# Four gate products in a row ahead of the latent attention, and sums of x formed later

## The chip, the core and the metric

The kernel runs on one core of a Trainium2 chip. The metric is the device time of one execution in microseconds (us), the median of several runs. TensorE (PE) multiplies; VectorE (DVE), ScalarE (ACT) and GpSimd (POOL) work beside it; SyncE (SP) issues the transfers of weights.

## What is computed

A trunk of two layers on 256 tokens of width 2048, all in float32. `u` is a normed copy of `x`, and `w_in` gives all the projections of a layer in one matrix: the latents of the latent attention (MLA), its rotary key, the queries, keys and values of a neighbourhood attention (NA), and two gates of width 2048.

```python
u = rmsnorm(x, norm_mix[l])
c_q, c_kv, k_pe, q_na, k_na, v_na, gate_a, gate_b = jnp.split(u @ w_in[l], IN_SPLITS, axis=-1)
y_a = mla_attention(...) @ w_o_mla[l]          # from c_q @ w_uq, c_kv @ w_ukv, k_pe
y_b = neighbourhood_attention(...) @ w_o_na[l]
merged = jax.nn.sigmoid(gate_a) * y_a + jax.nn.sigmoid(gate_b) * y_b
x = x + merged @ w_out[l]
h = rmsnorm(x, norm_mlp[l]) @ w_ff1[l]
x = x + jnp.square(jax.nn.relu(h)) @ w_ff2[l]
```

A final norm follows the second layer.

## The kernel before

**Weights and products.** Weights come as strips of up to 1 MB, tile `raw`, three buffers, issued by SyncE. Each strip is split into a rounded high part (`hi`, a cast on ScalarE, L176, L200) and the remainder (`lo`, a subtraction on VectorE, L177, L201); a product of two numbers is then three matmuls, high by high, high by low and low by high. Activations are split in the same way into a tile `pair` (L165 on ScalarE; L167 or L169 on VectorE). `gemm_a` (matmuls L231 to L233) and `gemm_b` (L222, L223) are plain products. `gemm_s` (L399) is a product with a Strassen scheme: strips numbered j in `pairs` are merged, with seven products of blocks in place of eight; the others are plain. A merged strip needs sums of the weights (tile `sums`, L445, L448 and L449 on VectorE) and sums of the activations, which `sums_of` makes by four additions of 128 columns (L348 to L351); `forms` (L353) calls it and splits the result (L358 on ScalarE, L359 on VectorE). A `gemm_s` ends with eight additions of banks (L464, VectorE) after a copy (L465 on ScalarE). Its matmuls are L413.

**What sets the order.** Every engine runs its own list in order; a tile framework waits for data and for buffers. Work that is not a step of a product (softmax heads, norms, transpositions, sums) sits in generators. `start(gen, lag)` puts one in `pending`, to be continued `lag` ticks later; `tick()`, called after every few matmuls, continues one that is due, or takes a head from `queued` when six ticks have passed since the last. `drain()` continues them all; `gemm_s` calls it at its first merged strip. `have()` continues the pending work until an activation exists. The scheduling of the framework then fixes the place of each instruction on its engine.

**A layer.** First half: the NA queries, keys and values; the latents C_Q and C_KV; the rotary key; the first gate product of gate b, here GB0 (1024 columns, `gemm_s`), the first two of the four products of `w_o_na` (512 columns each, `gemm_a`), GB1, the other two. Then the MLA stage: four rounds of `w_uq` and `w_ukv`, each of which queues two heads; the rotation is L516. Then GA0 (strips in the order LATE, three merged ones in a row), two products of `w_o_mla`, GA1, the other two. After each of these four a block of merged rows is complete (L777 and L778) and `turned` transposes it (matmuls L483), splits it and, for merged strips, calls `forms`. Second half: `w_out` as two `gemm_s`, then the feed-forward part, which ends with two `gemm_a` whose results are added to `x` (L866) and squared for the next norm (L328). At the end of a layer, and in layer 0's first product, `turned` does for `x` what it does for the merged rows.

**Buffers.** The two halves open and close pools of their own (`wpool`, `tmp`), so the second half's larger `hi` and `lo` tiles lie where the first half's were. In the first half the sums of the weights use the tag `pp`, two buffers, which the heads of attention use too (L548, L549).

Of the kernel before, what the change touches and what calls it, by code (L numbers as in the profile page):

```python
# [33 lines left out]
F32 = mybir.dt.float32  # L34
# [5 lines left out]
P = 128  # L40
# [27 lines left out]
MIXED, MERGED = (1, 2, 3), (1, 2, 3)  # L68
EARLY, LATE = [0, 4, 1, 5, 2, 6, 3, 7], [0, 4, 5, 6, 1, 3, 2, 7]

# [5 lines left out]
def trunk(ctx: ExitStack, tc: tile.TileContext, x, w_in, w_uq, w_ukv, rpb, w_o_mla, w_o_na,  # L76
# [3 lines left out]
    slots = ctx.enter_context(tc.tile_pool(name="slots", bufs=NSLOT))  # L80
    keep = ctx.enter_context(tc.tile_pool(name="keep", bufs=2))
    psum = ctx.enter_context(tc.tile_pool(name="psum", bufs=8, space=bass.MemoryType.PSUM))

    tmp = wpool = None
    hbufs, smalls, strips = HBUFS, SMALL, False
# [94 lines left out]
    def weights(w, nk, c0, n, before=None):  # L180
# [3 lines left out]
        for k0 in range(0, nk, 2):  # L184
            if before:
                before(k0)
            if k0 % step == 0:
                raw = wpool.tile([P, 2048], F32, tag="raw", name="raw", bufs=RBUFS)
                raw = raw[:, :step * n].rearrange("p (k n) -> p k n", n=n)
                nc.sync.dma_start(raw, w[k0 * P:(k0 + step) * P, c0:c0 + n].rearrange("(k p) n -> p k n", p=P))  # L190
                if strips:
                    his, los = (t.rearrange("p (k n) -> p k n", n=n) for t in parts(raw.rearrange("p k n -> p (k n)")))
# [11 lines left out]
    def weights_twice(w, nk, c0, n):  # L204

        raw = wpool.tile([P, 2048], F32, tag="raw", name="raw", bufs=RBUFS)
        raw = raw[:, :nk * n].rearrange("p (k n) -> p k n", n=n)
# [145 lines left out]

    def forms(f, sums, j):

        s = sums_of(f)
        h, lw = pair(), pair()
        nc.scalar.copy(h, s)  # L358
        nc.vector.tensor_tensor(lw, s, h.bitcast(F32), op=ALU.subtract)  # L359
        sums[j] = h, lw  # L360
        return
        yield

# [35 lines left out]
    def gemm_s(w, c0, get, order, pairs, evac):  # L399
# [23 lines left out]
        for j in order:  # L423
            raw = wpool.tile([P, 2048], F32, tag="raw", name="raw", bufs=RBUFS)
            nc.sync.dma_start(raw.rearrange("p (k n) -> p k n", n=1024),
# [13 lines left out]
            if strips:  # L439
                whole_ts = wpool.tile([P, 2048], F32, tag="sums", name="sums", bufs=1)  # L440
                ts = whole_ts[:, :1024], whole_ts[:, 1024:]
            else:
                ts = [tmp.tile([P, 1024], F32, tag="pp", name="sums", bufs=2) for _ in range(2)]
# [32 lines left out]
    def turned(src, c4, dst, scale, sums, pairs):  # L476


        for c in range(0, 4, 2):
# [18 lines left out]
            if j in pairs:  # L498
                start(forms(f, sums, j), 8)
            yield 1  # L500
# [124 lines left out]
    norm = RowNorm()  # L625
    xg, xs4 = [None] * NC, [None] * (NC // 2)

# [4 lines left out]
    def enter(k0):  # L632
# [4 lines left out]
        if k0 % 4 == 0:  # L637
            enter.gen = turned_x(k0 // 4, xg, G_MIX, xs4)
        next(enter.gen)
# [6 lines left out]
    for l in range(DEPTH):  # L646
# [43 lines left out]
        gemm_b(wi, C_Q, xg, latent(cq, nq, G_QA + 4 * l))  # L690
        start(nq.scales(), 10)
        gemm_b(wi, C_KV, xg, latent(ckv, nkv, G_KVA + 4 * l))
        start(nkv.scales(), 10)
# [8 lines left out]

        part = {}

        def gate(th):
            def evac(r):
                for i in range(2):
                    for t in range(2):
                        nc.scalar.activation(r[t, i], r[t, i], AF.Tanh, scale=mix.half[:, t:t + 1])
                th.update(r)  # L710
            return evac

        mixed = blocks(xg, xs4, MIXED)
        for g in range(2):
            th = {}
            gemm_s(wi, C_GB + g * 1024, mixed, EARLY, MIXED, gate(th))
            for i in range(2):
                def merge(t, ps):
                    m = part[t, 2 * g + i] = th[t, i]
                    nc.vector.scalar_tensor_tensor(m, m, 1.0, ps, op0=ALU.add, op1=ALU.mult)  # L720

                gemm_a(w_o_na[l], (2 * g + i) * 512, att_na, merge)

# [44 lines left out]

        mg, ms4 = [None] * NC, [None] * (NC // 2)
        for g in range(2):  # L770
            th = {}
            gemm_s(wi, C_GA + g * 1024, mixed, EARLY if g else LATE, MIXED, gate(th))
            for i in range(2):
                def merge(t, ps):
                    c4 = 2 * g + i
                    m, h = part[t, c4], th[t, i]
                    nc.vector.scalar_tensor_tensor(h, h, 1.0, ps, op0=ALU.add, op1=ALU.mult)  # L777
                    nc.vector.tensor_tensor(m, m, h, op=ALU.add)  # L778
                    if t == 1:
                        start(turned(lambda t: part[t, c4], c4, mg, lambda c: 0.5, ms4, MERGED), 2)  # L780

                gemm_a(w_o_mla[l], (2 * g + i) * 512, att, merge)
        half_a.close()
# [19 lines left out]
        for g in range(2):  # L803
# [10 lines left out]

            gemm_s(w_out[l], g * 1024, blocks(mg, ms4, MERGED), EARLY, MERGED, residual)
        mlp.scale()
# [12 lines left out]
        for b in range(NB):  # L829
# [31 lines left out]
            if b == NB - 1:  # L861
                rows = [[v[2 * k:2 * k + 2] for v in h] for h in hid for k in range(2)]
                for c4 in range(2, 4):
# [6 lines left out]
                    gemm_a(w2, c4 * 512, rows, residual3)  # L870
        xg, xs4 = nxt, nxt4
        if not last:
# [70 lines left out]
```

## Time and profile before

| | |
|---|---|
| median of 3 runs | 2681.57 us (2680.39 to 2682.54) |
| profiled execution | 2678.33 us |
| its span, first to last instruction | 2676.6 us |
| share of the span: TensorE, VectorE, ScalarE, GpSimd | 98%, 79%, 55%, 4% |
| mean granted clock of TensorE | 0.996 |
| moved by DMA | 508.95 MB, mean 190 GB/s |

In a row of a timeline stand the start in us, the length in us, engine, line, operation and output<-input tiles; in brackets the engine's idle time before it and what ended that. A matmul's length holds its latency too, so lengths overlap, and the pace is read from start to start. In a row of the list of waits stand the total, the number of waits and the longest. In a row of a window stand its bounds, its length, the busy time of PE, PE's weight loads, DVE, ACT and POOL with their counts, the granted clock of PE, the share of the DMA engines and GB/s. In a row of a group stand the count, then busy time and mean ns of one, then the idle time before.

### The profile page before, as it was taken

How to read it: one execution, taken by the hardware profiler on the slowest of the kernel's cores; microseconds unless marked ns; L12 is line 12 of the kernel's file. 1: busy time of each engine (PE TensorE's matmuls, PEld its weight loads, DVE VectorE, ACT ScalarE, POOL GpSimd, SP SyncE). 2: the span in 40 equal slices, each digit the busy share in tenths (PEclk: the TensorE clock that was granted, in tenths of full speed). 3: DMA queues.
4: the chain of work that ended last, by engine and by line, in shares of the span. 5: the costliest groups of instructions: out<-in, count | busy, mean ns of one | idle time of the engine just before them, and what ended most of it. 6: DMA issues, size and time to landing. Idle time of an engine off the chain costs nothing.

```text
span 2676.6 us, 32005 instructions
## 1 busy us (share of the span) xinstructions
PE 2624.5 (98%) x12498; PEld 2187.4 (82%) x12498; DVE 2126.3 (79%) x2496; ACT 1464.3 (55%) x1719; POOL 94.7 (4%) x117
## 2 busy tenths in 40 slices
PE   8999999999999999999999999999999999999998
PEld 6888887877888888888888888878788888888886
DVE  6778787878888887888767787978888888878885
ACT  6555565546554545545545555645565555455553
POOL 0100000000000010000001000000000000100000
PEclk9999999999999999999999999999999999999999
DMA  7555544565567575675555555445555665756744
GB/s 229 175 169 185 195 157 140 194 196 174 195 200 236 163 242 193 204 231 176 197 173 174 167 189 197 147 152 179 191 189 189 206 218 187 236 206 190 252 168 145
DMA packets 175256, 508.95 MB, mean 190 GB/s; under 512 B 13696, under 2 KB 18176, under 8 KB 175104
## 3 DMA queue, kind: packets, MB, share of 16 engines
q1 hardware_dynamic: 166192, 490.08, 55.0%
q0 software_dynamic: 8768, 16.78, 3.2%
q8 instruction: 98, 1.61, 0.2%
q14 instruction: 54, 0.44, 0.0%
q10 hardware_dynamic: 144, 0.04, 0.0%
HBM read 492.18 MB, written 2.10 MB: 185 GB/s over the span
## 4 chain that ended last, share of the span: by engine, by line
PE 68%; issue 21%; DVE 6%; ACT 3%; POOL 1%; DMA 1%; SPq 0%; POOLq 0%; ACTq 0%; DVEq 0%
PE bank L413 40%; PE bank L222 8%; PE bank L231 4%; PE bank L233 4%; PE bank L232 4%; PE bank L223 4%; DVE lo L177 3%; ACT hi L176 3%; PE bank L382 1%; DVE sums L445 1%; PE bank L238 1%; PE bank L237 1%; PE bank L236 1%; DMA raw<-in_w_in 1%; POOL xt L854 1%
## 5 line engine op out<-in xcount | busy, mean ns | idle before, releaser
L413 PE MATMUL bank<-hi,pair 128*128 128x512 f32 x5156 | 1614.8, 392 | 16.6 <-ACT hi L176 15.6
L413 PEld LDWEIGHTS bank<-hi,pair 128*128 128x128 f32 x5156 | 967.6, 188 | 229.8 <-ACT hi L176 32.9
L413 PE MATMUL bank<-lo,pair 128*128 128x512 f32 x2578 | 1010.6, 392 | 4.2 <-DVE lo L177 4.0
L176 ACT CAST hi<-raw 128x2048 fp32r<-128x2048 f32 (+3 forms) x416 | 633.3, 1534 | 435.0 <-PE bank L413 290.9
L177 DVE TENSOR_TENSOR lo<-raw,hi 128x2048 fp32r<-128x2048 f32 (+3 forms) x416 | 754.0, 1819 | 132.2 <-ACT hi L176 130.3
L413 PEld LDWEIGHTS bank<-lo,pair 128*128 128x128 f32 x2578 | 485.3, 188 | 110.0 <-DVE lo L177 11.4
L177 DVE TENSOR_TENSOR lo<-sums,hi 128x2048 fp32r<-128x2048 f32 (+1 forms) x134 | 255.9, 1910 | 162.3 <-ACT hi L176 161.9
L201 DVE TENSOR_TENSOR lo<-raw,hi 128x1024 fp32r<-128x1024 f32 (+1 forms) x224 | 270.2, 1213 | 134.0 <-ACT hi L200 133.1
L176 ACT CAST hi<-sums 128x2048 fp32r<-128x2048 f32 (+1 forms) x134 | 214.8, 1603 | 288.1 <-DVE sums L449 201.5
L222 PE MATMUL bank<-pair,hi 128*128 128x512 f32 x960 | 346.4, 403 | 9.7 <-ACT hi L200 6.0
L200 ACT CAST hi<-raw 128x1024 fp32r<-128x1024 f32 (+1 forms) x224 | 230.0, 1035 | 206.5 <-PE bank L222 81.1
L223 PE MATMUL bank<-pair,lo 128*128 128x256 f32 x960 | 267.8, 283 | 0.8 <-DVE lo L201 0.8
L222 PEld LDWEIGHTS bank<-pair,hi 128*128 128x128 f32 x960 | 181.3, 189 | 50.1 <-ACT hi L200 7.0
L232 PE MATMUL bank<-lo,pair 128*128 128x512 f32 (+1 forms) x576 | 218.1, 379 | 0.0
L233 PE MATMUL bank<-hi,pair 128*128 128x512 f32 (+1 forms) x576 | 217.7, 378 | 0.0
L464 DVE TENSOR_TENSOR wide<-wide,bank 128x512 f32<-128x512 f32 x336 | 215.7, 683 | 0.3 <-PE bank L413 0.3
L231 PE MATMUL bank<-hi,pair 128*128 128x512 f32 (+1 forms) x576 | 214.9, 379 | 0.0
L223 PEld LDWEIGHTS bank<-pair,lo 128*128 128x128 f32 x960 | 182.1, 190 | 2.6 <-DVE lo L201 1.1
L445 DVE TENSOR_TENSOR sums<-raw 128x1024 f32<-128x1024 f32 x110 | 134.4, 1221 | 21.2 <-DMA raw<-in_w_ff 14.7
L231 PEld LDWEIGHTS bank<-hi,pair 128*128 128x128 f32 x576 | 108.4, 188 | 20.2
L233 PEld LDWEIGHTS bank<-hi,pair 128*128 128x128 f32 x576 | 108.4, 188 | 19.9
L232 PEld LDWEIGHTS bank<-lo,pair 128*128 128x128 f32 x576 | 108.4, 188 | 19.4
(123 smaller groups left out, 1568.0 us busy)
## 6 DMA issues: line engine op xcount, KB each, us to landing
raw<-in_w_ff SPq DMA_DIRECT2D x256, 1024.0 KB, 5.3
raw<-in_w_in SPq DMA_DIRECT2D x124, 1024.0 KB, 5.1
raw<-in_w_out SPq DMA_DIRECT2D x32, 1024.0 KB, 5.3
raw<-in_w_o_na SPq DMA_DIRECT2D x16, 1024.0 KB, 5.0
raw<-in_w_o_mla SPq DMA_DIRECT2D x16, 1024.0 KB, 5.0
xt<-wide POOLq DMA_DIRECT2D x48, 256.0 KB, 7.2
raw<-in_w_ukv SPq DMA_DIRECT2D x8, 1024.0 KB, 4.9
raw<-in_w_uq SPq DMA_DIRECT2D x8, 768.0 KB, 4.4
```

The source lines that it names most:

```text
L176: nc.scalar.copy(hi, src)
L177: nc.vector.tensor_tensor(lo, src, hi.bitcast(F32), op=ALU.subtract)
L200: nc.scalar.copy(hi, src)
L201: nc.vector.tensor_tensor(lo, src, hi.bitcast(F32), op=ALU.subtract)
L222: nc.tensor.matmul(ps, wh, a, start=first, stop=False)
L223: nc.tensor.matmul(ps[:, :S], wl, a[:, :S], start=False, stop=last)
L231: nc.tensor.matmul(ps, ah, wh, start=first, stop=False)
L232: nc.tensor.matmul(ps, ah, wl, start=False, stop=False)
L233: nc.tensor.matmul(ps, al, wh, start=False, stop=last)
L413: nc.tensor.matmul(b[i], x, y, start=count[i] == 1, stop=count[i] == total[i])
L445: nc.vector.tensor_tensor(ts[0].rearrange("p (a n) -> p a n", a=2), raw[:, :512].rearrange("p (a n) -> p a n", a=1).to_broadcast([P, 2, 512]),
L464: add = lambda o, a, c: nc.vector.tensor_tensor(o, a, c, op=ALU.add)
```

## The change

The second half of `w_o_na` and the gate products change places: GB0, two products of `w_o_na`, then GB1, GA0 and GA1 one after the other, then the MLA stage, then the other two of `w_o_na` and all four of `w_o_mla`. All gate products take their strips in one order, `ORDER`, which is the old EARLY. The function `forms` now takes a list of blocks and makes their sums one after another, six ticks apart. For `x` it starts behind C_Q and no longer at each transposition; for the merged rows it starts behind the third of the four products of `w_o_mla`. `turned` starts with a lag of 4 in place of 2 there. The `raw` strips have one pool for the whole kernel, and the second half opens a pool of its own for the sums of weights ahead of the pool of `hi` and `lo`. The lines of the new kernel stand one below the old ones up to `forms` (L176 is L177), and eight below in the last part.

```diff
-EARLY, LATE = [0, 4, 1, 5, 2, 6, 3, 7], [0, 4, 5, 6, 1, 3, 2, 7]
+ORDER = [0, 4, 1, 5, 2, 6, 3, 7]
...
+    raws = ctx.enter_context(tc.tile_pool(name="raws", bufs=RBUFS))
...
-                raw = wpool.tile([P, 2048], F32, tag="raw", name="raw", bufs=RBUFS)
+                raw = raws.tile([P, 2048], F32, tag="raw", name="raw", bufs=RBUFS)
...
-    def forms(f, sums, j):
-
-        s = sums_of(f)
-        h, lw = pair(), pair()
-        nc.scalar.copy(h, s)
-        nc.vector.tensor_tensor(lw, s, h.bitcast(F32), op=ALU.subtract)
-        sums[j] = h, lw
-        return
-        yield
+    def forms(blocks, pairs, sums):
+
+        for j in pairs:
+            s = sums_of(blocks[j])
+            h, lw = pair(), pair()
+            nc.scalar.copy(h, s)
+            nc.vector.tensor_tensor(lw, s, h.bitcast(F32), op=ALU.subtract)
+            sums[j] = h, lw
+            yield 6
...
             if strips:
-                whole_ts = wpool.tile([P, 2048], F32, tag="sums", name="sums", bufs=1)
+                whole_ts = spool.tile([P, 2048], F32, tag="sums", name="sums", bufs=1)
...
             if j in pairs:
-                start(forms(f, sums, j), 8)
+                sums[j] = f
             yield 1
...
         gemm_b(wi, C_Q, xg, latent(cq, nq, G_QA + 4 * l))
         start(nq.scales(), 10)
+        xs4 = [None] * (NC // 2)
+        start(forms(xf4, MIXED, xs4), 10)
         gemm_b(wi, C_KV, xg, latent(ckv, nkv, G_KVA + 4 * l))
...
         mixed = blocks(xg, xs4, MIXED)
+        gemm_s(wi, C_GB, mixed, ORDER, MIXED, gate(part, 0))
+        local(0)
+        local(1)
+        gemm_s(wi, C_GB + 1024, mixed, ORDER, MIXED, gate(part, 1))
         for g in range(2):
-            th = {}
-            gemm_s(wi, C_GB + g * 1024, mixed, EARLY, MIXED, gate(th))
-            for i in range(2):
-                def merge(t, ps):
-                    m = part[t, 2 * g + i] = th[t, i]
-                    nc.vector.scalar_tensor_tensor(m, m, 1.0, ps, op0=ALU.add, op1=ALU.mult)
-
-                gemm_a(w_o_na[l], (2 * g + i) * 512, att_na, merge)
+            gemm_s(wi, C_GA + g * 1024, mixed, ORDER, MIXED, gate(other, g))
...
-        mg, ms4 = [None] * NC, [None] * (NC // 2)
-        for g in range(2):
-            th = {}
-            gemm_s(wi, C_GA + g * 1024, mixed, EARLY if g else LATE, MIXED, gate(th))
-            for i in range(2):
-                def merge(t, ps):
-                    c4 = 2 * g + i
-                    m, h = part[t, c4], th[t, i]
-                    nc.vector.scalar_tensor_tensor(h, h, 1.0, ps, op0=ALU.add, op1=ALU.mult)
-                    nc.vector.tensor_tensor(m, m, h, op=ALU.add)
-                    if t == 1:
-                        start(turned(lambda t: part[t, c4], c4, mg, lambda c: 0.5, ms4, MERGED), 2)
-
-                gemm_a(w_o_mla[l], (2 * g + i) * 512, att, merge)
+        local(2)
+        local(3)
+        mg, ms4, mf4 = [None] * NC, [None] * (NC // 2), [None] * (NC // 2)
+        for c4 in range(4):
+            def merge(t, ps):
+                m, h = part[t, c4], other[t, c4]
+                nc.vector.scalar_tensor_tensor(h, h, 1.0, ps, op0=ALU.add, op1=ALU.mult)
+                nc.vector.tensor_tensor(m, m, h, op=ALU.add)
+                if t == 1:
+                    start(turned(lambda t, c4=c4: part[t, c4], c4, mg, lambda c: 0.5, mf4, MERGED), 4)
+
+            gemm_a(w_o_mla[l], c4 * 512, att, merge)
+            if c4 == 2:
+                start(forms(mf4, MERGED, ms4), 4)
...
+        spool = half_b.enter_context(tc.tile_pool(name="spool", bufs=1, reuse_waits="tile"))
         wpool = half_b.enter_context(tc.tile_pool(name="wpool2", bufs=4, reuse_waits="tile"))
```

`local(c4)` is the `w_o_na` product with its merge, as it stood in the loop before. The lists below are the instructions of one engine in the order in which it runs them, without any times: line, operation, output<-input, shape and, after an x, how many in a row.

VectorE at the start of layer 0, before:

```order
L169 SCALAR_TENSOR_TENSOR pair<-bank,g_sb,pair 128x256 x2
L201 TENSOR_TENSOR lo<-raw,hi 128x1024 x2
L167 TENSOR_TENSOR pair<-wide,pair 128x256 x2
L348 TENSOR_TENSOR wide<-wide 128x128
L351 TENSOR_TENSOR wide<-wide 128x128
L349 TENSOR_TENSOR wide<-wide 128x128
L350 TENSOR_TENSOR wide<-wide 128x128
L201 TENSOR_TENSOR lo<-raw,hi 128x1024
L167 TENSOR_TENSOR pair<-wide,pair 128x256 x2
L359 TENSOR_TENSOR pair<-wide,pair 128x512
```

and after:

```order
L170 SCALAR_TENSOR_TENSOR pair<-bank,g_sb,pair 128x256 x2
L202 TENSOR_TENSOR lo<-raw,hi 128x1024 x2
L168 TENSOR_TENSOR pair<-wide,pair 128x256 x2
L202 TENSOR_TENSOR lo<-raw,hi 128x1024
L168 TENSOR_TENSOR pair<-wide,pair 128x256 x4
L170 SCALAR_TENSOR_TENSOR pair<-bank,g_sb,pair 128x256
L334 TENSOR_REDUCE var<-sums 128x2
```

The additions of `sums_of` and the subtraction behind them are gone from between the low parts of the strips.

VectorE at the start of GA0 before, where the sums of the weights stand among the work of the last heads (`pp` is a head's softmax, transposed; `small` and `pair` belong to a head's output):

```order
L445 TENSOR_TENSOR sums<-raw 128x1024
L549 TENSOR_TENSOR pp<-bank,pp 128x2x256
L167 TENSOR_TENSOR pair<-bank,pair 128x256
L177 TENSOR_TENSOR lo<-sums,hi 128x1024
L448 TENSOR_TENSOR sums<-raw,sums 128x512
L167 TENSOR_TENSOR pair<-bank,pair 128x256
L449 TENSOR_TENSOR sums<-raw,sums 128x512
L445 TENSOR_TENSOR sums<-raw 128x1024
```

and after, where L465 are the additions that end GB1, and the low parts and sums are those of GA0:

```order
L465 TENSOR_TENSOR wide<-wide,bank 128x512
L178 TENSOR_TENSOR lo<-raw,hi 128x1024 x2
L465 TENSOR_TENSOR wide<-wide,bank 128x512 x2
L178 TENSOR_TENSOR lo<-raw,hi 128x1024
L465 TENSOR_TENSOR wide<-wide,bank 128x512 x2
L446 TENSOR_TENSOR sums<-raw 128x1024
L465 TENSOR_TENSOR wide<-wide,bank 128x512
L178 TENSOR_TENSOR lo<-raw,hi 128x1024
L449 TENSOR_TENSOR sums<-raw,sums 128x512
```

The heads are gone from here, and the additions of the product before stand in their place.

VectorE at the opening of `w_out` before, from the last merge (L778) on:

```order
L778 TENSOR_TENSOR wide<-wide 128x512
L177 TENSOR_TENSOR lo<-raw,hi 128x2048 x2
L169 SCALAR_TENSOR_TENSOR pair<-bank,pair 128x256
L445 TENSOR_TENSOR sums<-raw 128x1024
L177 TENSOR_TENSOR lo<-raw,hi 128x1536
L169 SCALAR_TENSOR_TENSOR pair<-bank,pair 128x256 x2
L448 TENSOR_TENSOR sums<-raw,sums 128x512
```

and after (the last merge is L783):

```order
L446 TENSOR_TENSOR sums<-raw 128x1024
L349 TENSOR_TENSOR wide<-wide 128x128
L352 TENSOR_TENSOR wide<-wide 128x128
L783 TENSOR_TENSOR wide<-wide 128x512
L178 TENSOR_TENSOR lo<-raw,hi 128x2048
L449 TENSOR_TENSOR sums<-raw,sums 128x512
L350 TENSOR_TENSOR wide<-wide 128x128
L178 TENSOR_TENSOR lo<-raw,hi 128x2048
L170 SCALAR_TENSOR_TENSOR pair<-bank,pair 128x256
L178 TENSOR_TENSOR lo<-raw,hi 128x1536
L450 TENSOR_TENSOR sums<-raw,sums 128x512
```

The weights' sum and the first two additions of a merged row now stand ahead of the last merge, and more of those additions between the low parts.

More of the change, by code (lines that the diff above doesn't have):

```diff
@@ L81, in trunk @@
     keep = ctx.enter_context(tc.tile_pool(name="keep", bufs=2))
+    raws = ctx.enter_context(tc.tile_pool(name="raws", bufs=RBUFS))
     psum = ctx.enter_context(tc.tile_pool(name="psum", bufs=8, space=bass.MemoryType.PSUM))
-    tmp = wpool = None
+    tmp = wpool = spool = None
     hbufs, smalls, strips = HBUFS, SMALL, False
@@ L204, in weights_twice @@
     def weights_twice(w, nk, c0, n):
-        raw = wpool.tile([P, 2048], F32, tag="raw", name="raw", bufs=RBUFS)
+        raw = raws.tile([P, 2048], F32, tag="raw", name="raw", bufs=RBUFS)
         raw = raw[:, :nk * n].rearrange("p (k n) -> p k n", n=n)
@@ L423, in gemm_s @@
         for j in order:
-            raw = wpool.tile([P, 2048], F32, tag="raw", name="raw", bufs=RBUFS)
+            raw = raws.tile([P, 2048], F32, tag="raw", name="raw", bufs=RBUFS)
             nc.sync.dma_start(raw.rearrange("p (k n) -> p k n", n=1024),
@@ L625, in trunk @@
     norm = RowNorm()
-    xg, xs4 = [None] * NC, [None] * (NC // 2)
+    xg, xf4 = [None] * NC, [None] * (NC // 2)
     def load(c4):
@@ L637, in enter @@
         if k0 % 4 == 0:
-            enter.gen = turned_x(k0 // 4, xg, G_MIX, xs4)
+            enter.gen = turned_x(k0 // 4, xg, G_MIX, xf4)
         next(enter.gen)
@@ L700, in trunk, with gate @@
         start(rope(t, key_pe(ke)), 4)
-        part = {}
-        def gate(th):
+        part, other = {}, {}
+        def gate(th, g):
             def evac(r):
@@ L709, in evac, with local @@
                         nc.scalar.activation(r[t, i], r[t, i], AF.Tanh, scale=mix.half[:, t:t + 1])
-                th.update(r)
+                        th[t, 2 * g + i] = r[t, i]
             return evac
+        def local(c4):
+            def merge(t, ps):
+                m = part[t, c4]
+                nc.vector.scalar_tensor_tensor(m, m, 1.0, ps, op0=ALU.add, op1=ALU.mult)
+            gemm_a(w_o_na[l], c4 * 512, att_na, merge)
         mixed = blocks(xg, xs4, MIXED)
+        gemm_s(wi, C_GB, mixed, ORDER, MIXED, gate(part, 0))
+        local(0)
+        local(1)
+        gemm_s(wi, C_GB + 1024, mixed, ORDER, MIXED, gate(part, 1))
         for g in range(2):
-            th = {}
-            gemm_s(wi, C_GB + g * 1024, mixed, EARLY, MIXED, gate(th))
-            for i in range(2):
-                def merge(t, ps):
-                    m = part[t, 2 * g + i] = th[t, i]
-                    nc.vector.scalar_tensor_tensor(m, m, 1.0, ps, op0=ALU.add, op1=ALU.mult)
-                gemm_a(w_o_na[l], (2 * g + i) * 512, att_na, merge)
+            gemm_s(wi, C_GA + g * 1024, mixed, ORDER, MIXED, gate(other, g))
         att = [None] * HEADS
@@ L766, in trunk, with merge @@
                 queued.append(mla_head(h, qn[j], qr, kn[j], ke[j], vt, setter(att, h)))
-        mg, ms4 = [None] * NC, [None] * (NC // 2)
-        for g in range(2):
-            th = {}
-            gemm_s(wi, C_GA + g * 1024, mixed, EARLY if g else LATE, MIXED, gate(th))
-            for i in range(2):
-                def merge(t, ps):
-                    c4 = 2 * g + i
-                    m, h = part[t, c4], th[t, i]
-                    nc.vector.scalar_tensor_tensor(h, h, 1.0, ps, op0=ALU.add, op1=ALU.mult)
-                    nc.vector.tensor_tensor(m, m, h, op=ALU.add)
-                    if t == 1:
-                        start(turned(lambda t: part[t, c4], c4, mg, lambda c: 0.5, ms4, MERGED), 2)
-                gemm_a(w_o_mla[l], (2 * g + i) * 512, att, merge)
+        local(2)
+        local(3)
+        mg, ms4, mf4 = [None] * NC, [None] * (NC // 2), [None] * (NC // 2)
+        for c4 in range(4):
+            def merge(t, ps):
+                m, h = part[t, c4], other[t, c4]
[6 more added lines that the diff above has]
+                start(forms(mf4, MERGED, ms4), 4)
         half_a.close()
@@ L813, in residual @@
                                           2 * c4 + c in FIRST, gained(2 * c4 + c)), 4)
-            gemm_s(w_out[l], g * 1024, blocks(mg, ms4, MERGED), EARLY, MERGED, residual)
+            gemm_s(w_out[l], g * 1024, blocks(mg, ms4, MERGED), ORDER, MERGED, residual)
         mlp.scale()
@@ L870, in trunk @@
                     gemm_a(w2, c4 * 512, rows, residual3)
-        xg, xs4 = nxt, nxt4
+        xg, xf4 = nxt, nxt4
         if not last:
```

## The prediction

> **What bounds the kernel now.** I read the page's first part, then the list of waits, then the timeline of TensorE wherever its matmuls stop. A difference under 0.2% (5.4 us of 2681.57) cannot be told from no change here.
>
> ```profile
> PE 2624.5 (98%) x12498; PEld 2187.4 (82%) x12498; DVE 2126.3 (79%) x2496; ACT 1464.3 (55%) x1719; POOL 94.7 (4%) x117
> PE bank L413 <- ACT hi L176: 15.6, 28, 2.0
> PE bank L222 <- ACT hi L200: 6.0, 3, 2.5
> PE bank L413 <- DVE lo L177: 4.0, 9, 0.7
> PE bank L222 <- DVE pair L169: 3.7, 2, 2.3
> ```
>
> TensorE is busy 98% of the span and the change leaves its arithmetic as it is. So it is worth only the idle stretches it removes or makes, and there are few: the four waits above, all on the split of weights or activations, sum to 29.3 us. I go through the stretches where they lie. Matmuls of 512 columns follow each other every 0.22 to 0.23 us:
>
> ```profile
> 550.95 0.39 PE L232 MATMUL bank<-lo,pair 128*128 128x512 f32 x1
> 551.17 0.39 PE L233 MATMUL bank<-hi,pair 128*128 128x512 f32 x1
> 553.59 1.20 PE L413 MATMUL bank<-hi,pair 128*128 128x512 f32 x4 [2.03 <-ACT hi L176]
> 554.62 1.03 PE L483 MATMUL bank<-ident,wide 128*128 128x128 f32 x8
> 555.92 0.51 PE L413 MATMUL bank<-lo,pair 128*128 128x512 f32 x1 [0.26 <-DVE lo L177]
> 551.64 3.72 ACT L176 CAST hi<-raw 128x2048 fp32r<-128x2048 f32 x2 [1.32 <-PE bank L233]
> ```
>
> **Sums of x later: the opening of layer 0.** Idle stretches of TensorE there, and what VectorE does meanwhile:
>
> ```profile
> 27.33 0.49 PE L222 MATMUL bank<-pair,hi 128*128 128x512 f32 x1 [1.37 <-DVE pair L169]
> 31.27 0.50 PE L222 MATMUL bank<-pair,hi 128*128 128x512 f32 x1 [2.28 <-DVE pair L169]
> 34.33 0.50 PE L222 MATMUL bank<-pair,hi 128*128 128x512 f32 x1 [0.95 <-ACT hi L200]
> 35.62 0.39 PE L223 MATMUL bank<-pair,lo 128*128 128x256 f32 x1 [0.79 <-DVE lo L201]
> 15.76 2.17 POOL L585 TENSOR_TENSOR mb<-mb,mask_sb 128x384 f32<-128x384 f32 x2 [11.25 <-DMA mask_sb<-in_mask]
> 15.94 1.12 DVE L349 TENSOR_TENSOR wide<-wide 128x128 f32<-128x128 f32 x1
> 17.09 0.99 DVE L350 TENSOR_TENSOR wide<-wide 128x128 f32<-128x128 f32 x1
> 22.25 0.28 DVE L350 TENSOR_TENSOR wide<-wide 128x128 f32<-128x128 f32 x1
> 25.06 0.68 DVE L359 TENSOR_TENSOR pair<-wide,pair 128x512 fp32r<-128x512 f32 x1
> ```
>
> The four idle stretches sum to 5.4 us, and TensorE waits for VectorE directly or through a strip that VectorE frees late. Three sums (four additions of 0.28 us and one subtraction of 0.68, 1.8 us each, the first 1.6 more) stand among the strips' low parts. They hold up VectorE, so strip buffers come free late, so the next transfer starts late. Without them I find nothing late: 5.4 us gained. The lowest value is 2.5: the 2.28 and part of 0.95 stay if the strip's landing, not VectorE, sets that point. The most is 6.5, with the restarts.
>
> Where the sums go, behind C_Q, VectorE has room (first row below, 72% busy, TensorE at 60.00 of 60), so 5.4 us per layer of VectorE work is hidden there. If that cover were gone, the first gate would start later by up to 1.8 us, the last sum; I take 0.
>
> ```profile
> 140.00:200.00 60.00, 60.00 (x336) 52.24 (x335) 43.18 (x77) 33.43 (x61) 5.46 (x6) 1.00 0.53 167
> 433.00:458.00 25.00, 21.26 (x87) 15.09 (x86) 20.36 (x24) 13.41 (x18) 0.00 (x0) 0.93 0.33 104
> 553.00:582.00 29.00, 28.15 (x127) 23.19 (x128) 23.96 (x20) 15.57 (x13) 0.00 (x0) 1.00 0.57 182
> ```
>
> One rule speaks against this move. While GpSimd's two additions ran (15.76 to 17.93), the additions of 128 columns took 1.12 and 0.99 us against 0.28. The Trainium skill ("SBUF — State Buffer", section "SBUF: two separate sides") says that VectorE with two SBUF inputs and GpSimd take a shared pair of ports as an exclusive lock, the other blocking for the whole instruction; the trace agrees with it in those two rows. By that rule the strip's low part, which now comes next, would meet the same GpSimd work and wait up to 1.1 us, and the gain would be 4.3, the time 1.1 us higher. I don't take it, because TensorE's first long idle stretch comes ten microseconds later.
>
> **Layer boundary.** In the timeline of ScalarE and TensorE at the end of layer 0:
>
> ```profile
> 1342.35 0.63 ACT L328 ACTIVATE junk<-xt 128x512 bf16<-128x512 f32 x1 [0.64 <-DVE xt L866]
> 1342.98 3.87 ACT L200 CAST hi<-raw 128x1024 fp32r<-128x1024 f32 x4
> 1344.06 1.49 PE L222 MATMUL bank<-pair,hi 128*128 128x512 f32 x4 [2.53 <-ACT hi L200]
> 1345.34 1.91 PE L483 MATMUL bank<-ident,xt 128*128 128x128 f32 x8
> ```
>
> The first strip's split stands behind the second square of x. In the new order it stands ahead of it, so it starts 1.2 us earlier and the wait of 2.5 falls to 1.3. Behind that wait the matmuls ran slower: four took 1.28 us up to the next row where 0.23 each makes 0.92, and eight transpositions are 1.91 us long against 1.03 in the row at 554.62; that is 1.2 us. I take it that a wait of half the length leaves them at full pace: 2.4 gained (1.2 if not, 0 if the split isn't earlier).
>
> **Gates together: the third gate product.** Today GA0 starts with attention heads woven in and three merged strips in a row (LATE).
>
> ```profile
> 434.28 0.69 DVE L549 TENSOR_TENSOR pp<-bank,pp 128x512 fp32r<-128x512 f32 x1 [4.42 <-ACT pp L548]
> 436.90 1.23 DVE L445 TENSOR_TENSOR sums<-raw 128x1024 f32<-128x1024 f32 x1 [1.93 <-PE bank L238]
> 438.78 0.39 PE L237 MATMUL bank<-pp,pair 128*128 128x256 f32 x1 [0.71 <-DVE pp L549]
> 440.51 0.50 PE L413 MATMUL bank<-lo,pair 128*128 128x512 f32 x1 [0.42 <-DVE lo L177]
> 443.18 2.17 PE L413 MATMUL bank<-hi,pair 128*128 128x512 f32 x4 [1.47 <-ACT hi L176]
> 456.15 0.73 PE L413 MATMUL bank<-hi,pair 128*128 128x512 f32 x2 [0.52 <-ACT hi L176]
> L413 PE MATMUL bank<-hi,pair 128*128 128x512 f32 x46 | 17.1, 433 | 2.4 <-ACT hi L176 2.2
> L413 PE MATMUL bank<-lo,pair 128*128 128x512 f32 x21 | 9.0, 426 | 0.5 <-DVE lo L177 0.4
> ```
>
> VectorE idles 4.42 and 1.93 us because the sums' buffers (tag "pp") are held by the heads; then it has all merged strips to do at once, and TensorE waits four times; the granted clock of that window is 0.93. The 25 us hold 67 matmuls of 512 columns (15.2 us at 0.227), 12 of 256 at about half and 8 of 128 at about a quarter (2.3, an estimate from that pace): 7.5 us are lost. Now GA0 follows GB1 with neither heads nor LATE, the new order puts the low parts of its first strips between the additions that end GB1, and its sums' buffers are free. I take all 7.5 per layer (5 at least, if the eight additions that close a product delay the next one's first low part). Heads move into the last two products of w_o_na, where nine or more matmuls lie between two steps of a head: 0. w_o_na, w_o_mla and their strips keep size and number; SyncE's issues only change order, in the one queue, three strips ahead as now.
>
> **Start of the latent attention.** It now follows GA1's combining instead of a w_o_na product.
>
> ```profile
> L464 DVE TENSOR_TENSOR wide<-wide,bank 128x512 f32<-128x512 f32 x56 | 35.9, 684 | 0.0
> 353.23 0.42 DVE L244 TENSOR_TENSOR small<-bank,small 128x256 f32<-128x256 f32 x1
> 355.28 0.96 DVE L201 TENSOR_TENSOR lo<-raw,hi 128x768 fp32r<-128x768 f32 x1 [0.17 <-ACT hi L200]
> ```
>
> By the new order TensorE has, from GA1's last matmul on, 23 matmuls of w_uq (12 of 512 columns, 11 of 256: 4.0 us) before the rotation's product, which waits for VectorE. VectorE then still has about three and a half additions at 0.6, a low part of 1.1, three small steps of 0.35 and the low part of 0.9: 5.2 us. So 1.2 us are lost per layer (0 to 2.5).
>
> **Opening of w_out.** The sums of the merged rows now come in its first strips, not ahead of it.
>
> ```profile
> L445 DVE TENSOR_TENSOR sums<-raw 128x1024 f32<-128x1024 f32 x21 | 25.6, 1221 | 3.2 <-PE bank L238 1.9 <-DMA raw<-in_w_in 1.2
> L177 DVE TENSOR_TENSOR lo<-raw,hi 128x2048 fp32r<-128x2048 f32 x19 | 43.2, 2287 | 2.3 <-ACT hi L176 2.3
> ```
>
> Before, TensorE loses 2.2 us for the first strip's high part, whose buffer lies over one still read, and 0.3 behind it: 2.5. After: the high part (1.9) starts 0.8 us before the last matmul of w_o_mla, because that buffer is free earlier, and 0.9 is lost. The transpositions of the last block then wait for VectorE, which has the weights' sum (1.22) and two small additions ahead of the last merge: 1.85. The first low part (2.29) follows: 1.1. Then three strips and the sums (1.8 each) are due within 16 us of matmuls on VectorE; the fourth strip's low part comes 2.5 late. Together 6.35, so 3.8 lost per layer (0 if VectorE's order bends, 6 if the restarts add up). After 2.03 idle layer 0 kept its pace here; with 3.85 idle within 6 us I take the slow matmuls of 1.2 us too.
>
> **Sum.** Opening -5.4, boundary -2.4; layer 0: -7.5 + 1.2 + 3.8 + 1.2 = -1.3; layer 1, where w_out's opening may slow already: -7.5 + 1.2 + 3.8 = -2.5. Together -11.6. The profiled execution took 2678.33, its span 2676.6; it becomes 2666.7. It lies 3.2 under the median, so the median becomes 2670.0.
>
> **Rivals.**
> First, w_out's opening loses nothing more than today: VectorE is 83% busy at 553 to 582, so 5 us of room are there. Then 3.8 twice and 1.2 come back: 2661. Against it, the order puts the sums ahead of the low parts. 0.12.
> Second, the opening of layer 0 stays tied to the landing of strips, 2.9 less: 2673. For it, transfers there start when a buffer is free. 0.09.
> Third, no change: GA0's loss goes only half, since part belongs to three merged strips and VectorE's load, not to the heads (7.5 kept over two layers), and the sums behind C_Q delay the first gate by 1.8 per layer: -11.6 + 7.5 + 3.6 = -0.5, 2681. 0.16.
> Fourth, slower: VectorE falls behind at the borders of gates that stand directly together. Eight additions at 0.6 make 4.8 us; where they all come ahead of the next product's first low part, TensorE waits that long, at three borders (GB1 to GA0, GA0 to GA1, GA1 to the attention) and in two layers: 28.8, less the 2.4 counted, so 2670 + 26.4 = 2696. It decides from about half of the additions standing ahead (2684). For it, VectorE is the second busiest; against it, the new order has low parts between the additions. 0.08.
>
> **Chances.** The forecast 0.55, rivals 0.12, 0.09, 0.16, 0.08. Faster is 0.55 + 0.12 + 0.09 = 0.76, same 0.16, slower 0.08. The range runs from 2659, w_out free and the opening at its most, to 2681, the third rival; the slower case is left out.
>
> **What would show it.** Right: no wait of matmuls on VectorE's pairs in the first 36 us; TensorE full over GA0 with granted clock 1.00; a wait of about 1.3 at the layer boundary; about 1 us before the rotation's first product; three or four waits in w_out's first 25 us, 6 us in all. Wrong: waits on low parts at the borders of the gates, or idle TensorE ahead of the first gate.

## The result, and the profile after

The changed kernel takes 2664.78 us (median of 4 runs, 2664.43 to 2665.67) against 2682.06 before (4 runs, 2680.39 to 2683.45): a ratio of 0.9936, interval 0.9919 to 0.9954. That is 17.3 us less; 11.6 were forecast. The profiled execution's span is 2662.8 us against 2676.6, 13.8 less.

The page of the changed kernel, and its list of waits of TensorE:

```profile
PE 2616.6 (98%) x12498; PEld 2181.1 (82%) x12498; DVE 2121.3 (80%) x2496; ACT 1461.4 (55%) x1719; POOL 94.8 (4%) x117
...
PE bank L414 <- ACT hi L177: 9.1, 24, 0.5
PE bank L414 <- DVE lo L178: 7.7, 11, 1.4
...
PE bank L517 <- DVE small L741: 4.1, 4, 1.5
PE bank L223 <- ACT hi L201: 3.7, 2, 2.5
PE bank L484 <- DVE wide L783: 3.3, 4, 1.2
```

The waits for ScalarE's high parts fell from 15.6 to 9.1 and from 6.0 to 3.7, and the wait for VectorE's pairs (3.7) is gone. Longer are those for low parts, 7.7 (4.0 before), and for the rotation's input (L517), 4.1 (1.5 before); new is 3.3 for the last merge (L783). These are what the change paid.

Idle time is less than half of the gain. Span less busy time of TensorE was 52.1 us and is 46.2, 5.9 less; the busy time itself fell by 7.9 for the same 12498 matmuls, so they stood closer together. In four windows of the profile before, the granted clock was at half (in a row: bounds, length, busy us and count of PE, weight loads, DVE, ACT and POOL, PE's clock, DMA share, GB/s):

```profile
443.70:447.10 3.40, 3.28 (x8) 2.42 (x8) 3.40 (x5) 1.85 (x3) 0.00 (x0) 0.50 0.73 284
1344.80:1348.20 3.40, 3.40 (x15) 3.00 (x15) 3.40 (x5) 2.42 (x4) 2.28 (x2) 0.50 0.00 0
1771.40:1774.80 3.40, 3.40 (x9) 2.66 (x9) 3.40 (x6) 0.42 (x1) 0.00 (x0) 0.51 0.35 140
1880.70:1884.10 3.40, 3.40 (x13) 2.92 (x12) 3.40 (x2) 2.70 (x3) 0.00 (x0) 0.50 0.32 36
```

They lie in GA0 of each layer, at the layer boundary and at the opening of `w_out` in layer 1, each behind waits. After, the clock is 1.00 from 30 to 2650 us. Half speed for 3.4 us costs at most 1.7, so the four make at most 6.8 of the 13.8 us: an estimate from these rows, and for this pair of executions only. At `w_out` it was 1.1: from the last matmul ahead of it to the same later one, layer 1 took 6.63 us (1877.48 to 1884.11), layer 0 at full clock 5.57 (551.17 to 556.74).

To see where the time went, the kernel is cut at six places that every version has: (A) the matmul ahead of GB0's first wait for a low part in layer 0, (B) the last matmul ahead of `w_out`, (C) the matmul ahead of the feed-forward part's first wait, then A, B and C again in layer 1. All are starts in the timeline of TensorE, in us; the columns are differences.

| | to A | A to B | B to C | C to A, layer 1 | A to B, layer 1 | B to C, layer 1 |
|---|---|---|---|---|---|---|
| before | 235.95 | 315.22 | 122.70 | 888.38 | 315.23 | 122.61 |
| after | 229.76 | 310.28 | 126.44 | 884.48 | 310.18 | 125.33 |
| x_sums_alone | 230.24 | 315.24 | 122.24 | 887.33 | 315.24 | 122.58 |
| pools_alone | 240.43 | 315.27 | 122.54 | 884.64 | 315.21 | 122.55 |
| gates_alone | 239.72 | 310.75 | 127.70 | 888.15 | 310.25 | 126.55 |
| third_gate_early | 238.14 | 311.19 | 122.58 | 887.50 | 311.89 | 122.66 |
| gates_back | 229.10 | 311.61 | 124.54 | 884.58 | 312.07 | 124.51 |
| merged_sums_first | 229.60 | 310.13 | 122.93 | 884.50 | 310.54 | 123.19 |
| w_o_na_ahead | 229.04 | 309.31 | 127.17 | 884.47 | 309.41 | 127.11 |
| gates_back_sooner | 228.77 | 312.85 | 124.32 | 884.58 | 312.73 | 125.92 |
| first_one_between | 229.66 | 308.34 | 124.15 | 884.54 | 308.28 | 124.10 |

So the opening gained 6.2 us, the stretch from GB0 to `w_out` 4.9 and 5.1, the layer boundary (inside C to A) 3.9, and the opening of `w_out` (inside B to C) lost 3.7 and 2.7.

The opening after, as a window of 20 us:

```profile
24.00:44.00 20.00, 20.00 (x118) 17.56 (x117) 15.49 (x27) 11.30 (x20) 0.00 (x0) 1.00 0.82 266
```

The same window before:

```profile
24.00:44.00 20.00, 14.60 (x82) 12.05 (x81) 13.28 (x23) 9.32 (x16) 0.00 (x0) 1.00 0.70 223
```

TensorE is full where it had been busy for 14.60 of 20, with 118 matmuls in place of 82. The transfers follow: 266 GB/s in place of 223. They were late because VectorE gave the buffers back late, not the other way round: the run with the sums of x alone, below, changes only when these sums are made.

The four gate products in a row, after, in two windows that hold the borders GB1 to GA0 and GA0 to GA1:

```profile
280.00:345.00 65.00, 65.00 (x288) 53.85 (x287) 52.88 (x58) 34.19 (x38) 0.00 (x0) 1.00 0.57 200
345.00:400.00 55.00, 55.00 (x244) 45.53 (x244) 47.21 (x51) 33.00 (x38) 0.00 (x0) 1.00 0.57 197
```

TensorE has no idle time in either, with VectorE at 81% and 86%. The start of the latent attention after, on TensorE and VectorE:

```profile
410.31 0.94 DVE L202 TENSOR_TENSOR lo<-raw,hi 128x768 fp32r<-128x768 f32 x1
411.18 0.41 DVE L741 TENSOR_TENSOR small<-small,rrow 128x256 f32<-128x256 f32 x1
411.65 0.70 PE L517 MATMUL bank<-small,turn 128*128 128x256 f32 x2 [1.48 <-DVE small L741]
```

The rotation waits for a small product on VectorE, which stands behind GA1's additions and a low part. The layer boundary after, on ScalarE and TensorE:

```profile
1333.63 0.63 ACT L329 ACTIVATE junk<-xt 128x512 bf16<-128x512 f32 x1 [10.15 <-DVE xt L874]
1334.26 3.88 ACT L201 CAST hi<-raw 128x1024 fp32r<-128x1024 f32 x4
1335.34 1.19 PE L223 MATMUL bank<-pair,hi 128*128 128x512 f32 x4 [1.18 <-ACT hi L201]
1336.37 1.03 PE L484 MATMUL bank<-ident,xt 128*128 128x128 f32 x8
```

The splits follow the first square, the wait fell from 2.53 to 1.18, and the matmuls behind it run at full pace: four in 1.03 us from start to start, eight transpositions 1.03 long against 1.91. The opening of `w_out` after:

```profile
540.97 1.20 PE L414 MATMUL bank<-hi,pair 128*128 128x512 f32 x4 [0.54 <-ACT hi L177]
543.63 0.88 PE L484 MATMUL bank<-ident,wide 128*128 128x128 f32 x6 [1.25 <-DVE wide L783]
545.83 0.50 PE L414 MATMUL bank<-lo,pair 128*128 128x512 f32 x1 [0.90 <-DVE lo L178]
562.50 0.50 PE L414 MATMUL bank<-lo,pair 128*128 128x512 f32 x1 [1.43 <-DVE lo L178]
```

These are the four waits that the prediction counted, in its order. VectorE's rows there show what stands ahead of the first low part:

```profile
541.35 1.22 DVE L446 TENSOR_TENSOR sums<-raw 128x1024 f32<-128x1024 f32 x1
542.48 0.28 DVE L349 TENSOR_TENSOR wide<-wide 128x128 f32<-128x128 f32 x1
...
542.89 0.69 DVE L783 TENSOR_TENSOR wide<-wide 128x512 f32<-128x512 f32 x1
543.49 2.28 DVE L178 TENSOR_TENSOR lo<-raw,hi 128x2048 fp32r<-128x2048 f32 x1
```

### The profile page after: what moved, and what is told of

It reads as the page before. It is cut to its first block, busy times and chain, and to the rows that moved or that the text cites. A ratio compares the mean times of both kernels' runs of the same rounds, so it can differ in the third digit from the quotient of the medians.

```text
span 2662.8 us, 31999 instructions
## 1 busy us (share of the span) xinstructions
PE 2616.6 (98%) x12498; PEld 2181.1 (82%) x12498; DVE 2121.3 (80%) x2496; ACT 1461.4 (55%) x1719; POOL 94.8 (4%) x117
## 4 chain that ended last, share of the span: by engine, by line
PE 68%; issue 21%; DVE 6%; ACT 3%; POOL 1%; DMA 0%; POOLq 0%; DVEq 0%; ACTq 0%; SPq 0%
PE bank L414 40%; PE bank L223 8%; PE bank L224 4%; PE bank L232 4%; PE bank L233 4%; PE bank L234 4%; DVE lo L178 3%; ACT hi L177 2%; PE bank L383 1%; PE bank L239 1%; PE bank L238 1%; PE bank L237 1%; DVE wide L465 1%; DVE sums L446 1%; POOL xt L862 1%
## 5 line engine op out<-in xcount | busy, mean ns | idle before, releaser
L177 ACT CAST hi<-raw 128x2048 fp32r<-128x2048 f32 (+3 forms) x416 | 632.4, 1534 | 433.8 <-PE bank L414 302.4
L177 ACT CAST hi<-sums 128x2048 fp32r<-128x2048 f32 (+1 forms) x134 | 214.8, 1603 | 286.1 <-DVE sums L450 185.0
L465 DVE TENSOR_TENSOR wide<-wide,bank 128x512 f32<-128x512 f32 x336 | 215.3, 678 | 0.1
```

The source lines that it names most:

```text
L177: nc.scalar.copy(hi, src)
L465: add = lambda o, a, c: nc.vector.tensor_tensor(o, a, c, op=ALU.add)
```

## The experiments

**The sums of x alone.** The kernel before, in which only the sums of x start behind C_Q:

```diff
-            if j in pairs:
+            if j in pairs and late:              # late is True for x
+                sums[j] = f
+            elif j in pairs:
                 start(forms(f, sums, j), 8)
...
         start(nq.scales(), 10)
+        xs4 = [None] * (NC // 2)
+        start(forms_all(xf4, MIXED, xs4), 10)
```

> The kernel before with one part of the change: the sums of x formed behind C_Q, all else as it was. Theory: the four idle stretches of TensorE between 25 and 36 us go, and GB0 starts 6.2 us earlier as in the changed kernel; the wait at the layer boundary (2.7 us and slow matmuls) stays, because it hangs on which buffers the first strip's high part lies over, not on the sums; total about 6 us less. First rival: the landing of strips sets the opening, then 2.5 less. Second rival: the sums of x make the boundary's gain too, then about 10 less.

Measured: 2670.26 us against 2681.12, ratio 0.9961 (0.9946 to 0.9976). Mark A is 5.7 us earlier, C to A 1.05 shorter, all else within 0.5 of before. The theory holds for the trace of the opening; the landing of strips is not what bound it. The wait at the boundary stays:

```profile
1337.91 1.25 PE L222 MATMUL bank<-pair,hi 128*128 128x512 f32 x4 [2.53 <-ACT hi L200]
```

So the second rival fails by the trace, though the median fell by 10.9, near its figure and more than the 7.3 of the span. A likely reason for the difference stands in the executions that keep the old opening: they reach A at 235.95, 240.43, 239.72 and 238.14 in four profiles, those with the new one at 228.77 to 230.24 in seven. The window of the opening in pools_alone, the slowest of them:

```profile
24.00:44.00 20.00, 13.96 (x58) 11.09 (x57) 12.16 (x22) 8.00 (x14) 0.00 (x0) 0.74 0.65 211
```

The granted clock is 0.74 there and 1.00 in the window of before: the same stage sometimes lost the clock behind its waits and sometimes did not. The profile of before was a good draw, so a sum made against it was too small in this term. The record of 25 executions of the kernel before fits: eight with a mean granted clock of 0.996 average 2679.7 us, fifteen with 0.995 2681.4, two with 0.994 2682.7.

**The pools alone.** The kernel before with the pool `raws` and the pool `spool` ahead of `wpool` in the second half:

```diff
+    raws = ctx.enter_context(tc.tile_pool(name="raws", bufs=RBUFS))
...
+        spool = half_b.enter_context(tc.tile_pool(name="spool", bufs=1, reuse_waits="tile"))
         wpool = half_b.enter_context(tc.tile_pool(name="wpool2", bufs=4, reuse_waits="tile"))
```

> The kernel before with only the pools of the change: one pool of strips for the whole kernel, and a pool for the sums ahead of the pool of high and low parts in the second half. Theory: the layer boundary falls by 3 to 4 us (wait of 1.3 in place of 2.7, matmuls behind it at full pace), and at the opening of w_out the first high part starts earlier, its wait 0.9 in place of 2.2, in both layers; total 5 to 7 less. Rival: the pools only move addresses, the order of ScalarE at both places comes from the sums; then nothing changes, within 1 us.

Measured: 2678.91 against 2681.12, ratio 0.9993 (0.9984 to 1.0002): not to be told from no change in the median, and the interval holds 3.7 us less too. In the stages it is clear: C to A in layer 1 is 3.7 us shorter, and over the whole table the seven kernels with these pools take 884.47 to 884.64 there, the four without 887.33 to 888.38. So the boundary's gain comes from the pools; which of the two makes it was not run. At `w_out` the theory's half failed:

```profile
556.69 1.19 PE L414 MATMUL bank<-hi,pair 128*128 128x512 f32 x4 [0.60 <-ACT hi L177]
558.77 0.87 PE L484 MATMUL bank<-ident,wide 128*128 128x128 f32 x6 [0.67 <-DVE wide L779]
560.97 0.50 PE L414 MATMUL bank<-lo,pair 128*128 128x512 f32 x1 [1.33 <-DVE lo L178]
```

The high part is earlier, 0.60 in place of 2.03, but then the next two waits show, for VectorE, which the long one had hidden. B to C stays at 122.5.

**The gates alone.** The kernel before with the products reordered (as in the diff of the change, with the old `forms`, its lag of 2 for `turned`, and the old pools).

> The kernel before with only the products reordered: all four gate products ahead of the latent attention, the second half of w_o_na behind it, one order of strips; sums of x and of the merged rows and the pools as they were. Theory: the 7.5 us at the start of GA0 go in each layer, the start of the latent attention loses 1.9, the opening of w_out keeps its 2.5: 5.6 less per layer, 11 in all. Rival: half of GA0's loss comes back at the borders between the gate products, which now stand directly together: 4 less in all.

Measured: 2680.24, ratio 0.9996 (0.9986 to 1.0005). A to B is 4.5 and 5.0 us shorter, less than the 5.6 of the theory; a part of what is missing is a transposition of merged rows that waits 0.40 us at 526. But B to C is 5.0 and 3.9 us longer, which neither the theory nor the rival had. ScalarE and TensorE there:

```profile
552.99 0.62 ACT L358 CAST pair<-wide 128x512 fp32r<-128x512 f32 x1 [1.95 <-DVE wide L350]
...
553.79 1.89 ACT L176 CAST hi<-raw 128x2048 fp32r<-128x2048 f32 x1
...
555.73 1.65 PE L413 MATMUL bank<-hi,pair 128*128 128x512 f32 x3 [4.87 <-ACT hi L176]
```

The cast of a merged row's sums stands ahead of the first strip's split and waits for VectorE; TensorE waits 4.87 us, and from 554.0 to 560.8 the granted clock is 0.50. So the reordering by itself gives back at `w_out` what it gains. With the later sums and the pools of the change the loss there is 3.7 and 2.7; how much each of the two makes of that was not run.

**The third gate in the early order.** The kernel before, with one order of strips for both GA products:

```diff
-            gemm_s(wi, C_GA + g * 1024, mixed, EARLY if g else LATE, MIXED, gate(th))
+            gemm_s(wi, C_GA + g * 1024, mixed, EARLY, MIXED, gate(th))
```

> The kernel before with GA0 in the order of strips of the other gates, the heads still woven into it. Theory: what holds GA0 up is that the heads hold the two buffers of the sums of weights and stand among VectorE's work there; with the other order VectorE gets some room, and of 7.5 us per layer at most 2.5 go. Rival: the three merged strips in a row are the cause; then 6 or more of the 7.5 go in each layer, 12 in all.

Measured: 2674.95, ratio 0.9977 (0.9968 to 0.9987). A to B is 4.0 and 3.3 us shorter. The theory and the rival both missed: it lies between. What is left of GA0's loss, in the window and on TensorE:

```profile
425.00:450.00 25.00, 22.41 (x108) 17.98 (x107) 22.48 (x31) 15.35 (x22) 0.00 (x0) 1.00 0.40 129
```

```profile
431.68 0.73 PE L413 MATMUL bank<-hi,pair 128*128 128x512 f32 x2 [1.41 <-ACT hi L176]
433.40 0.73 PE L413 MATMUL bank<-hi,pair 128*128 128x512 f32 x2 [0.99 <-ACT hi L176]
```

The clock holds at 1.00 where before it had fallen to half, an estimated 1.7 at most of the 4.0 and 3.3, and two waits remain, behind the last heads. So three merged strips in a row made about half of the loss. The other half goes with the heads: with the gates back, below, the same two waits stand (1.41 and 0.97), and in the changed kernel, where no heads run beside GA0, they are gone.

**The gates back.** The changed kernel with the products in the order of before, everything else of the change kept:

```diff
         gemm_s(wi, C_GB + 1024, mixed, ORDER, MIXED, gate(part, 1))
-        for g in range(2):
-            gemm_s(wi, C_GA + g * 1024, mixed, ORDER, MIXED, gate(other, g))
+        local(2)
+        local(3)
...
-        local(2)
-        local(3)
...
+            if c4 % 2 == 0:
+                gemm_s(wi, C_GA + c4 * 512, mixed, ORDER, MIXED, gate(other, c4 // 2))
             gemm_a(w_o_mla[l], c4 * 512, att, merge)
```

> The changed kernel with the order of products of before (GB0, two of w_o_na, GB1, two of w_o_na, latent attention, GA0 with heads woven in, two of w_o_mla, GA1, two of w_o_mla); one order of strips, sums and pools as in the change. Theory, from the run with GA0 in the early order: the reordering itself keeps 3.5 us at GA0 and pays 1.9 at the start of the latent attention, the opening of w_out is the same, so this is 1.5 slower per layer, 3 in all, near 2668. Rival: the reordering carries the whole 7.5 of GA0: then 5 or more slower per layer, near 2676.

Measured: 2665.51 (2663.76 to 2668.55) against 2664.78 of the change; their ratios to the kernel before are 0.9943 (0.9928 to 0.9957) and 0.9936 and their ranges overlap, so the two can't be told apart. The stages agree with the theory in sign: A to B is 1.3 and 1.9 longer than after; B to C is 1.9 and 0.8 shorter, which the theory had not. What the change is named for, gates in a row, is worth about nothing once GA0 has the early order.

**The merged sums first.** The changed kernel, two numbers:

```diff
-            if c4 == 2:
-                start(forms(mf4, MERGED, ms4), 4)
+            if c4 == 0:
+                start(forms(mf4, MERGED, ms4), 8)
```

> The changed kernel with the sums of the merged rows started behind the first product of w_o_mla instead of the third, so that all three are formed ahead of w_out. Theory: VectorE's 5.4 us of sums are what makes the opening of w_out lose 3.7 and 2.7 us more than before; with them gone the late low part of the fourth strip (1.6 and 1.4 us) and part of the first waits go: 2 to 3.5 less per layer, 4 to 7 in all, near 2660. Rival: the sums' cast on ScalarE then stands ahead of the first strip's split, as in the run with the gates alone, and TensorE waits there up to 5 us: no gain, or slower.

Measured: 2659.66 (2658.95 to 2660.22), ratio to before 0.992 (0.9903 to 0.9936); 5.1 us under the change, and its range lies apart from the change's. B to C is 122.93 and 123.19, 3.5 and 2.1 shorter than after. TensorE at the opening of `w_out`:

```profile
540.90 1.19 PE L414 MATMUL bank<-hi,pair 128*128 128x512 f32 x4 [0.78 <-ACT hi L177]
543.14 0.88 PE L484 MATMUL bank<-ident,wide 128*128 128x128 f32 x6 [0.83 <-DVE wide L783]
545.34 0.50 PE L414 MATMUL bank<-lo,pair 128*128 128x512 f32 x1 [0.77 <-DVE lo L178]
```

The fourth strip's late low part (1.43) is gone, the waits ahead of it are a little shorter in sum. B to C is now 0.2 and 0.6 longer than before the change, so it was VectorE's sums in this place that cost most of the 3.7 and 2.7 us.

**Sums sooner with the gates back.** The run with the gates back, with `c4 == 1` in place of `c4 == 2`.

> The same with the sums of the merged rows started behind the second product of w_o_mla, so that they are formed during GA1 and the last two products. Theory: the opening of w_out falls from 6.3 us of waits to about 3, so 3 less per layer than the run with the gates back, near 2662, and under the changed kernel: the best order then needs no reordering. Rival: the sums on VectorE during GA1 delay its low parts by as much: the same as the run with the gates back, within 1 us.

Measured: 2668.03 (2667.45 to 2668.32), ratio 0.995 (0.9936 to 0.9965): 2.5 slower than the gates back. The theory fails and the rival holds, with more than it said. TensorE in GA1 and at `w_out`:

```profile
437.54 0.50 PE L414 MATMUL bank<-lo,pair 128*128 128x512 f32 x1 [1.22 <-DVE lo L178]
...
544.53 0.87 PE L484 MATMUL bank<-ident,wide 128*128 128x128 f32 x6 [1.39 <-DVE wide L781]
546.73 0.50 PE L414 MATMUL bank<-lo,pair 128*128 128x512 f32 x1 [1.32 <-DVE lo L178]
```

A wait for a low part appears some 105 us ahead of `w_out`, which the gates back do not have, and the first waits at `w_out` are fewer but longer: A to B is 1.2 and 0.7 longer than with the gates back, B to C 0.2 shorter and 1.4 longer. Work moved on VectorE is free only where VectorE has room.

**A product of w_o_na ahead of the attention.** The changed kernel, with `local(2)` moved between GA1 and the latent attention.

> The changed kernel with the third product of w_o_na put between GA1 and the latent attention. Theory: the wait of 1.64 us and the 0.4 of slower starts behind it come from GA1's closing additions on VectorE; a plain product between gives them time, so 1.8 less per layer, 3.6 in all, near 2661. Rival: the heads of the latent attention have only one product of w_o_na left to run beside before w_o_mla needs them, and TensorE waits for the last heads: 2 or more lost per layer, no gain or slower.

Measured: 2664.53 (2661.78 to 2664.78): no gain, the rival's result, but only in small part by its cause. TensorE:

```profile
432.64 0.67 PE L517 MATMUL bank<-small,turn 128*128 128x256 f32 x2 [0.56 <-DVE small L742]
498.51 0.39 PE L237 MATMUL bank<-pp,pair 128*128 128x256 f32 x1 [0.53 <-ACT pp L549]
539.99 1.21 PE L414 MATMUL bank<-hi,pair 128*128 128x512 f32 x4 [1.25 <-ACT hi L177]
```

The wait of 1.48 ahead of the first rotation is gone (the longest left is 0.56, in the second round), but a head waits 0.53, the first high part at `w_out` 1.25 in place of 0.54, and slow matmuls follow (545 to 548): A to B is 1.0 and 0.8 shorter than after, B to C 0.7 and 1.8 longer. So the heads did not take the gain, as the rival had it; the opening of `w_out` did.

**One product between, sums first.** The merged sums first, and `local(1)`, which stood behind `local(0)`, between GA1 and the attention:

```diff
         local(0)
-        local(1)
         gemm_s(wi, C_GB + 1024, mixed, ORDER, MIXED, gate(part, 1))
         for g in range(2):
             gemm_s(wi, C_GA + g * 1024, mixed, ORDER, MIXED, gate(other, g))
+        local(1)
```

> The changed kernel with the sums of the merged rows started behind the first product of w_o_mla, and the second product of w_o_na (not the third) put between GA1 and the latent attention, so that two products of w_o_na still stand behind the attention and cover its last heads. Theory: the wait of 1.6 us at the start of the latent attention goes as in the run with a product ahead of it, and the waits that run paid for it (0.7 us for a head, a later first high part at w_out) stay away: 1.8 less per layer than the run with the merged sums first, near 2656. Rival: the waits at the start of the latent attention turn up elsewhere on VectorE; then within 1 us of 2659.7.

Measured: 2656.59 (2654.7 to 2657.35), ratio 0.9907 (0.9891 to 0.9924), the fastest here: 8.2 us under the change. The list of waits of TensorE:

```profile
PE bank L414 <- DVE lo L178: 4.4, 8, 0.8
...
PE bank L484 <- DVE wide L783: 2.4, 4, 0.8
PE bank L517 <- DVE small L741: 1.5, 4, 0.6
```

A to B is 1.9 shorter than after in both layers. The wait of the rotation fell from 4.1 to 1.5 and that for low parts from 7.7 to 4.4, with no wait for a head. Against the merged sums first, A to B is 1.8 and 2.3 shorter, as the theory had it, but B to C is 1.2 and 0.9 longer; in layer 0 the granted clock falls to 0.50 there (543.5 to 546.9).

## Why the prediction was right

The forecast was 2670.0 in a range of 2659 to 2681; measured 2664.78. By its own steps:

- *Opening, 5.4.* Right in place and cause; 6.2 in the profiles and about 9 against the mean of four executions with the old opening (238.6 against 229.4 of seven with the new). This term was too small: the prediction took the loss from one profile in which the clock happened to hold.
- *The rule of the shared ports* from the Trainium skill ("SBUF — State Buffer", section "SBUF: two separate sides") foretold that the strip's low part would now wait for GpSimd. VectorE and GpSimd of the changed kernel, where it did:

```profile
15.84 1.99 POOL L586 TENSOR_TENSOR mb<-mb,mask_sb 128x384 f32<-128x384 f32 x2 [11.34 <-DMA mask_sb<-in_mask]
17.14 1.77 DVE L202 TENSOR_TENSOR lo<-raw,hi 128x1024 fp32r<-128x1024 f32 x1 [1.21 <-ACT hi L201]
```

  The low part took 1.77 us where others take 1.22, 0.55 more: by that rule, the trace agrees; TensorE has no wait there, so it cost nothing, as taken.
- *Boundary, 2.4.* Measured 3.9, of which the pools alone make 3.7: the wait by 1.35, the rest from the matmuls behind it, at half clock from 1344.8 to 1348.2 and a little slower for some 40 us after, where the prediction counted twelve. This term was too small as well.
- *GA0, 7.5 per layer.* The loss is gone. But the step gave the whole of it to the gates standing together; 4.0 and 3.3 of it come with the order of strips alone, and the third rival, which said so, had that mechanism right though not its result. In the step's own sum the 20 smaller matmuls come to 1.8 by its halves and quarters, not 2.3, which would make 8.0.
- *Start of the attention, 1.2 lost.* 1.6 from start to start, and 0.4 in slower starts behind it. The step took VectorE's additions at 0.6; the row that it shows has a mean of 684 ns, and with that its sum gives 1.4.
- *A wait that the sum has at nothing.* The transpositions of merged rows wait for VectorE once in each layer ahead of `w_out`, where they did not before:

```profile
515.55 0.44 PE L484 MATMUL bank<-ident,wide 128*128 128x128 f32 x2 [0.40 <-DVE wide L783]
```

  So A to B was forecast 6.3 shorter in each layer and is 4.9 and 5.1: the one stage in which the change gained less than forecast.
- *Opening of w_out, 3.8 lost, and 1.2 of slow matmuls in layer 0.* 3.7 and 2.7; the slow matmuls did not come in the profiled execution. Layer 1 lost less, by the 1.1 that the half clock had cost there before, as the sum had it. The four waits counted are 4.1 us in sum, not 6.35; the rest of the loss lies in the starts behind them and in shorter waits.
- *The change is worth only idle stretches*, as the first paragraph had it. 7.9 of the 13.8 us are pace and not idle time; the steps for GA0 and the boundary held a part of that, the first paragraph did not.

Of the rivals, w_out at no loss and the opening tied to landing are out by the stages; VectorE falling behind at the borders of the gates (2696) is out by the two full windows. The third's other half, a first gate held up by the sums behind C_Q, did not come: from 20 to 280 us TensorE has two waits, 0.5 and 0.4, which it had before as well.

The sum of the profile was 11.6 against 13.8 measured, and it is that near partly by luck: the opening, the boundary and `w_out` came out 4.7 better than forecast, A to B 2.6 worse. The 3.5 us between the span's and the median's gain fit the varying old opening, which is argued from seven and four profiles and not shown for each of the runs timed.

## What to carry to other kernels

A profile of one execution can be a lucky draw in a stage that stalls: the runs that differ elsewhere and share the stage give its spread. When a change is a bundle, its parts should be run alone: here the sums of x (10.9 us alone) and the order of strips in one gate (6.2 alone) come to about the whole gain of 17.3, though no run has just these two together, and the reordering that the change is named for makes about none, since it gives back at `w_out` and at the attention what it saves. Work that a busy VectorE does for a later product is best put where the windows show room ahead of it, not into the product's own opening, and not into another product that is full.

## What the runs showed of the hardware

The granted clock of TensorE fell after groups of short waits, and not always after the same ones. In the run with a product of `w_o_na` ahead of the attention, waits of 1.25, 0.74 and 0.70 us within five were followed by slow matmuls:

```profile
544.00:549.00 5.00, 4.64 (x13) 3.69 (x14) 5.00 (x6) 0.00 (x0) 0.00 (x0) 0.66 0.71 219
```

After the 0.54, 1.25 and 0.90 of the changed kernel they were not. Nor is it the size of the waits alone: at the same place, with waits of 0.78, 0.81 and 0.77, the clock of the run with one product between fell to 0.50 (543.5 to 546.9), and with 0.78, 0.83 and 0.77 that of the merged sums first stayed at 1.00 (545.3 to 552). The Trainium skill ("TensorE: Matmul & The Clock Gate", section "Why this matters for your kernels") asks for no idle gap over about 3 us; here the clock fell with no single gap above 1.3, so staying under that figure was not enough. The Trainium skill ("TensorE: Matmul & The Clock Gate", section "What's actually happening") puts the cause in an activity window that runs free, which fits the old opening, the same program text, at 1.00 in one execution and 0.74 in another kernel's.
